# Two-layer recurrent/attention trunk on one Trainium2 core: squares' sums and conditioning rows as one-column matrix products, last gate unit ahead of the last two recurrence blocks, conditioning rows spread over other steps

## The chip, the cores and the metric

The kernel runs on one core of one Trainium2 chip. The core has five engines, each with its own queue: TensorE (PE) multiplies matrices, VectorE (DVE) and ScalarE (ACT) work element by element, GpSimd (POOL) does odd work, and SyncE (SP) issues most of the DMAs. PE writes its results to PSUM, eight banks of 128 x 512 numbers here. The time is the device time of one execution in microseconds; the value shown of a kernel is the median of its runs.

## The reference

Input are `x` (1024 positions x 1024 features, float32), one vector `c` of 1024 numbers, and the parameters. Everything is float32. Layer 0 is a recurrent mixer and an MLP; then one key/value pair is computed; layer 1 is chunked attention and an MLP. What the change touches is the first norm with its conditioning, and the mixer:

```python
c_act = jax.nn.silu(c)
mod = c_act @ ada_w[layer] + ada_b[layer]
sh1, sc1, g1, sh2, sc2, g2 = jnp.split(mod, 6, axis=-1)
hn = modulate(rms_norm(h, norm1_g[layer]), sh1, sc1)
...
z = hn @ w_in
gate, xr = jnp.split(z, 2, axis=-1)
xr = causal_depthwise_conv(xr, conv_w, conv_b)
y = rg_lru(xr, gate_a_w, gate_a_b, gate_x_w, gate_x_b, lam)
return (y * jax.nn.gelu(gate)) @ w_out
```

`rms_norm` divides each position by the root of the mean of its 1024 squares; `modulate` is x * (1 + scale) + shift, with `scale` and `shift` taken from the 6144 numbers `mod`. The mixer is 1408 wide. `rg_lru` works on 16 blocks of 88 features: two 88 x 88 products with sigmoids, elementwise work, and a scan over the 1024 positions. The MLP is `square(relu(hn @ w1)) @ w2`, 4096 wide.

## The kernel before

All activations lie with features on the partitions: eight tiles of 128 features x 1024 positions, each position half 512 wide. Every float32 product is made of three of reduced precision: both operands are split into a high part (written by ACT, `hi`) and a low part (the rest, subtracted by DVE, `lo`), and PE accumulates three products, weight-high x moving-high (L324), weight-high x moving-low (L325) and weight-low x moving-high (L326), in this order. One *unit* is 128 output features: 8 k-tiles x 2 halves x 3 = 48 products of 512 columns.

Weights come through one stream (`ws`). Its items are loaded by SP in order, split by ACT (L191) and DVE (L195), and freed. Conditioning rows are items of that stream too: a *row* is 128 of the 6144 outputs of `mod`, its weights lie as 128 outputs x 1024 inputs, and one DVE instruction (L357) multiplies them by silu(c), broadcast to all partitions as `cb`, and adds up along the row, writing one column of `mods`. Which rows come between which weights is written by hand (`some`, `ada_late`). In the mixer and the first MLP a counter of ticks decides when delayed jobs and low halves are issued (`ws.tick`, `ws.late`, `ws.flush`). The order on each engine is the order of the code there.

**Head.** Squares of x (ACT, L516 and L519) are added up over the eight k-tiles by DVE (L520); four products with a column of ones per half sum them over the partitions (L528); DVE and ACT take the reciprocal root (L533, L619 to L624), DVE writes it on a diagonal (L538), PE broadcasts it (L544), and ACT copies it from PSUM. DVE multiplies x by it (`normed`, L779), ACT applies gain and shift and makes the high half (`moded`, L786 and L788), DVE the low half (`lows`, L792). The 16 rows of scale and shift, two per k-tile, are reduced on DVE (L357) just ahead of their k-tile. Behind this stand the products of the first three units over both halves, 144 of them (`products`).

**Mixer.** For t = 3 to 10: a recurrent unit `xr(t)` with its convolution, the recurrence of the blocks that are complete (`recur`), then a gate unit (`gate(t-1)`). `recur` consists of, per block, 4 x 3 products of 88 x 88 (`gates`; their operands come by DMA and are split at L900 on ACT and L907 on DVE), sigmoids (L933), then tanh, square root and exponential on ACT (L945, L950, L953), and five DVE instructions that end with the scan (L957 to L961). The results go through DRAM (`ygd`) and come back as operands of the output projection, three chunks of k-tiles, whose PSUM banks DVE evicts with the gated residual (L1059).

**First MLP.** Its first four units of `w1` wait for the second norm, hidden tile by hidden tile (`head`; L583 scales, ACT adds the shift and makes the high half, L601 is the low half). The other 28 go in fourteen *quads* of two units (q = 2 to 15), with seven products of half matrices in place of eight; conditioning rows are put between them.

## Time and profile before

| | |
|---|---|
| median of three runs | 2389.01 us (2387.49 to 2394.32) |
| profiled execution | 2395.81 us |
| span of its profile | 2394.0 us |
| mean granted clock of PE | 0.985 |
| PE busy | 2287.7 us |
| DVE busy | 1763.6 us |
| ACT busy | 1246.2 us |

The profiled execution is 6.8 us longer than the median of the runs and has 1.8 us outside its span. In the rows of a timeline the first number is the start in us, the second the duration; then come engine, line, operation, the tile written and the tiles read, the shape and the count; in brackets the idle time of the engine before it and what ended it. In a row of windows each engine has its busy time and its number of instructions, in the order PE, weight loads of PE, DVE, ACT, POOL, followed by the granted clock, the DMA share and GB/s.

### The profile page before, as it was taken

How to read it: one execution, taken by the hardware profiler on the slowest of the kernel's cores; microseconds unless marked ns; L12 is line 12 of the kernel's file. 1: busy time of each engine (PE TensorE's matmuls, PEld its weight loads, DVE VectorE, ACT ScalarE, POOL GpSimd, SP SyncE). 2: the span in 40 equal slices, each digit the busy share in tenths (PEclk: the TensorE clock that was granted, in tenths of full speed). 3: DMA queues.
4: the chain of work that ended last, by engine and by line, in shares of the span. 5: the costliest groups of instructions: out<-in, count | busy, mean ns of one | idle time of the engine just before them, and what ended most of it. 6: DMA issues, size and time to landing. Idle time of an engine off the chain costs nothing.

```text
span 2394.0 us, 31739 instructions
## 1 busy us (share of the span) xinstructions
PE 2287.7 (96%) x11740; PEld 1935.6 (81%) x11740; DVE 1763.6 (74%) x2596; ACT 1246.2 (52%) x2052; POOL 398.7 (17%) x419
## 2 busy tenths in 40 slices
PE   4999989999999899999999999999999999899999
PEld 3778767878877777888999998998888888778887
DVE  8797779588777777778765648997386666778775
ACT  5677873265544643334443229997165555634342
POOL 0001000000000023331000038875000000033322
PEclk9999989999999999999999999999999999999999
DMA  8343349326666774546244200013214444865443
GB/s 306 101 133 106 104 120 314 109 69 220 245 227 236 267 268 147 161 146 228 88 145 131 96 10 10 10 37 122 95 45 165 169 158 163 285 238 161 155 149 133
DMA packets 141640, 363.46 MB, mean 152 GB/s; under 512 B 14924, under 2 KB 17100, under 8 KB 141484
## 3 DMA queue, kind: packets, MB, share of 16 engines
q1 hardware_dynamic: 113756, 278.45, 35.3%
q10 hardware_dynamic: 23824, 71.44, 7.8%
q0 software_dynamic: 3904, 11.54, 1.9%
q8 instruction: 92, 1.51, 0.3%
q14 instruction: 64, 0.52, 0.1%
HBM read 260.19 MB, written 89.65 MB: 146 GB/s over the span
## 4 chain that ended last, share of the span: by engine, by line
PE 65%; DVE 13%; DMA 9%; ACT 8%; issue 4%; POOL 1%; SPq 0%; ACTq 0%; DVEq 0%; POOLq 0%
PE b L325 20%; PE b L326 20%; PE b L324 20%; DMA ws<-in_w_dram 3%; DVE wl L195 2%; DMA hid<-s 2%; PE b L1568 1%; DVE s L195 1%; ACT s L1538 1%; DVE s L357 1%; DMA ws<-hid 1%; ACT s L329 1%; DVE s L1129 1%; POOL ws L123 1%; PE b L1587 1%
## 5 line engine op out<-in xcount | busy, mean ns | idle before, releaser
L324 PE MATMUL b<-s,wh 128*128 128x512 f32 (+1 forms) x2532 | 1004.2, 397 | 43.3 <-DVE s L1231 11.7
L325 PE MATMUL b<-s,wh 128*128 128x512 f32 (+1 forms) x2532 | 998.7, 394 | 19.4 <-DVE s L907 6.5
L326 PE MATMUL b<-s,wl 128*128 128x512 f32 (+1 forms) x2296 | 905.4, 394 | 4.1 <-DVE wl L195 4.1
L324 PEld LDWEIGHTS b<-s,wh 128*128 128x128 f32 (+1 forms) x2532 | 480.0, 190 | 165.0 <-DVE s L1209 13.9
L325 PEld LDWEIGHTS b<-s,wh 128*128 128x128 f32 (+1 forms) x2532 | 479.8, 189 | 128.1 <-DVE s L907 7.4
L191 ACT ACTIVATE wh<-ws 128x1024 fp32r<-128x1024 f32 (+2 forms) x302 | 291.1, 973 | 441.6 <-POOL ws L123 261.1
L326 PEld LDWEIGHTS b<-s,wl 128*128 128x128 f32 (+1 forms) x2296 | 435.1, 190 | 100.1 <-DVE wl L195 5.8
L195 DVE TENSOR_TENSOR wl<-ws,wh 128x1024 fp32r<-128x1024 f32 (+2 forms) x249 | 305.8, 1231 | 113.8 <-ACT wh L191 111.5
L1231 DVE SCALAR_TENSOR_TENSOR s<-b,mod,s 128x512 f32<-128x512 f32 x221 | 165.0, 747 | 88.3 <-PE b L326 88.0
L195 DVE TENSOR_TENSOR s<-ws,s 128x512 fp32r<-128x512 f32 x284 | 223.4, 805 | 0.3 <-ACT s L191 0.3
L123 POOL TENSOR_TENSOR ws<-ws 128x512 f32<-128x512 f32 x21 | 28.4, 1354 | 1165.2 <-DMA s<-hsp 922.3
L324 PE MATMUL b<-wh,s 128*128 128x256 f32 x768 | 216.4, 284 | 0.0
L325 PE MATMUL b<-wl,s 128*128 128x256 f32 x768 | 216.0, 283 | 0.0
L326 PE MATMUL b<-wh,s 128*128 128x256 f32 x768 | 215.2, 283 | 0.5 <-DVE s L562 0.4
L191 ACT ACTIVATE s<-ws 128x512 fp32r<-128x512 f32 x284 | 165.1, 619 | 73.4 <-DMA ws<-ygd 23.7
L325 PEld LDWEIGHTS b<-wl,s 128*128 128x128 f32 x768 | 147.1, 192 | 0.3 <-issue 0.2
L324 PEld LDWEIGHTS b<-wh,s 128*128 128x128 f32 x768 | 147.1, 192 | 0.3 <-issue 0.2
L326 PEld LDWEIGHTS b<-wh,s 128*128 128x128 f32 x768 | 146.5, 192 | 1.0 <-DVE s L562 0.9
L357 DVE CUSTOM_DVE_ANT_0 ws<-ws,cb,vec 128x1024 f32<-128x1024 f32 x59 | 75.3, 1282 | 76.1 <-DMA ws<-in_ada_dram 73.3
L1209 DVE TENSOR_TENSOR s<-s,b 128x512 f32<-128x512 f32 x84 | 57.5, 685 | 99.9 <-PE b L326 88.1
L1207 ACT ACTIVATE s<-b 128x512 f32<-128x512 f32 x84 | 50.0, 596 | 93.2 <-PE b L326 93.0
L1338 ACT ACTIVATE s<-b 128x256 f32<-128x256 f32 x96 | 31.6, 388 | 121.5 <-PE b L326 110.3
(165 smaller groups left out, 3083.7 us busy)
## 6 DMA issues: line engine op xcount, KB each, us to landing
hid<-s ACTq DMA_DIRECT2D x128, 512.0 KB, 5.3
ws<-hid SPq DMA_DIRECT2D x118, 512.0 KB, 4.5
ws<-in_w_dram SPq DMA_DIRECT2D x220, 256.0 KB, 3.4
ws<-in_ada_dram SPq DMA_DIRECT2D x56, 512.0 KB, 3.5
s<-in_ada_dram SPq DMA_DIRECT2D x40, 512.0 KB, 8.8
ws<-in_w_in_dram SPq DMA_DIRECT2D x22, 512.0 KB, 4.6
hsp<-s SPq DMA_DIRECT2D x32, 256.0 KB, 2.0
s<-hsp SPq DMA_DIRECT2D x16, 512.0 KB, 6.9
```

Source lines behind the costliest of these rows:

```text
L123: eng.tensor_tensor(out=out, in0=in0, in1=in1, op=op)
L191: self.nc.scalar.activation(out=hi[:rows, :n], in_=src, func=AF.Copy)
L195: self.nc.vector.tensor_tensor(out=lo[:rows, :n], in0=src, in1=hi[:rows, :n].bitcast(F32), op=ALU.subtract)
L324: PE.matmul(ps, ah, bh, start=start, stop=False, skip_group_check=more)
L325: PE.matmul(ps, ah, bl, start=False, stop=False, skip_group_check=more)
L326: return PE.matmul(ps, al, bh, start=False, stop=stop, skip_group_check=more).ins
L329: A_.activation(out=hi, in_=src, func=AF.Copy)
L357: V.tensor_tensor_reduce(out=t, in0=t, in1=cb, op0=ALU.mult, op1=ALU.add, scale=1.0, scalar=bias, accum_out=dst)
L1207: A_.activation(out=t, in_=ps, func=AF.Copy)
L1209: V.tensor_tensor(out=t, in0=t, in1=ps, op=ALU.add)
L1231: V.scalar_tensor_tensor(out=t, in0=ps, scalar=g2[:, m : m + 1], in1=t, op0=ALU.mult, op1=ALU.add)
L1338: A_.activation(out=d, in_=ps[:, :, e * 128 : (e + 1) * 128], func=AF.Copy)
```

## The change

In the **head** the squares are no longer added up by DVE. Each k-tile's square is multiplied by the column of ones, 4 products per k-tile, all 32 of a half accumulating in one PSUM bank (`sums`). For the conditioning rows of the first norm the weights of a row also exist in another layout (`ada0`: 1024 inputs on the partitions, in eight blocks of 128 x 128), so that eight products with silu(c) as a 128 x 8 tile (`silu`) accumulate one row in one PSUM column (`ada_pe`). Both rows go this way for k = 0, 1, 2, the shift row alone for k = 3 to 7; the scale row of k = 3 to 7 stays on DVE. The load of `cb` and its silu come later.

In the **mixer** the rows between the units are 3, 3, 2 at t = 4, 6, 8 (before 2 each at t = 3 to 6), and the last gate unit (`gate(NT - 1)`) stands ahead of the recurrence of blocks 14 and 15; its weights are loaded ahead of the last gate blocks'. In the **first MLP**, the low halves that are due are written out at the start of each step of the first four units (`ws.flush()`), and the quads carry 0 rows at q = 2 and 15, 2 at q = 3, 8, 13, 14 and 3 elsewhere: 32 instead of 37. The eight rows of the key/value shift go to the **query stage**, four each after the second and third group of weights.

```diff
-        some(2 if t < 7 else 0)
+        some({4: 3, 6: 3, 8: 2}.get(t, 0))
...
     w_in(NT - 2)
+    w_in(NT - 1)
     gate_item(_done(NT - 1))
-    w_in(NT - 1)
...
-            ada_late(0 if l or q == 2 else 2 if q in (3, 15) else 3)
+            ada_late(0 if l or q in (2, 15) else 2 if q in (3, 8, 13, 14) else 3)
...
     for g in range(4):
         for kk in range(2):
             ws.add(I["wq"][g * 2 + kk], 1024)
+        some((0, 4, 4, 0)[g])
...
     load_x(0)
-    nc.sync.dma_start(cb, I["c"].broadcast_to([128, 1024]))
...
     ws.load(3)
+    nc.sync.dma_start(cb, I["c"].broadcast_to([128, 1024]))
...
-    for k in range(KD):
-        n1.sq(k, hs(0))
...
+    def sums(half):
+
+        n1.ps = bank()
+        for k in range(KD):
+            t = slot()
+            A_.activation(out=t[:, :HALF], in_=xt[k][:, hs(half)], func=AF.Square)
+            for j in range(4):
+                PE.matmul(n1.ps[:, j : j + 1], t[:, j * 128 : (j + 1) * 128], ones[:, 0:1],
+                          start=(k, j) == (0, 0), stop=(k, j) == (KD - 1, 3))
+
+    def ada_pe(k):
+
+
+        ps = bank()
+        todo = (1, 0) if k < 3 else (0,)
+        ts = {j: st.pop(0) for j in (1, 0)}
+        for j in todo:
+            for i in range(KD):
+                PE.matmul(ps[:, j : j + 1], ts[j][:, i * 128 : (i + 1) * 128], silu[:, i : i + 1],
+                          start=i == 0, stop=i == KD - 1)
+
+        def out():
+            if k > 2:
+                ada_use(mods[0][:, 8 + k : 9 + k], vc("ab0", 8 + k))(ts[1])
+            for j in todo:
+                V.tensor_tensor(out=mods[0][:, j * 8 + k : j * 8 + k + 1], in0=ps[:, j : j + 1],
+                                in1=vc("ab0", j * 8 + k), op=ALU.add)
+            gain(0, mods[0], 1, vc("n1g0", k), k, 1)
+        return out
...
     gate(NT - 2)
-    recur(_done(NT - 1))
...
     gate(NT - 1)
+    recur(_done(NT - 1))
     load_h(4)
...
+            ws.flush()
             head(k, nrm, l == 0)
```

Added lines push most line numbers up: what is L324, L325, L326 before is L325, L326, L327 after; L195 becomes L196, L357 L358, L520 L521, L544 L551, L601 L608, L907 L938, L957 L988, L1059 L1090. The sums' products are now L779, the rows' L790.

PE, start of the program. Before: four products sum the squares of half 0 (L528), one broadcasts (L544), six are the first k-tile's of two units.

```order
L528 MATMUL b_207<-ones,s_181 128x1 x4
L544 MATMUL b_230<-s_220,ones 128x512
L324 MATMUL b_275<-s_239,wh_222 128x512
L325 MATMUL b_275<-s_240,wh_222 128x512
L326 MATMUL b_275<-s_239,wl_223 128x512
```

After (of the eight rows of L779, which read alike, the last two):

```order
L779 MATMUL b_185<-ones,s_222 128x1 x4
L779 MATMUL b_185<-ones,s_228 128x1 x4
L790 MATMUL b_244<-silu,s_106 128x1 x8
L790 MATMUL b_244<-silu,s_108 128x1 x8
L551 MATMUL b_269<-s_242,ones 128x512
L790 MATMUL b_282<-silu,s_114 128x1 x8
L790 MATMUL b_282<-silu,s_116 128x1 x8
L325 MATMUL b_299<-s_277,wh_261 128x512
L326 MATMUL b_299<-s_278,wh_261 128x512
```

Six more rows of L779, one per k-tile, stand ahead of this piece. The rows of the first two k-tiles stand around the broadcast, ahead of the first 512-column product.

DVE, around the last recurrence (blocks 14 and 15) and the first evictions of the output projection. Before, the first chain of L957 to L961 for these blocks ends ahead of the first eviction L1059:

```order
L957 SCALAR_TENSOR_TENSOR s_2424<-s_2364,s_2424 88x1024
L958 SCALAR_TENSOR_TENSOR s_2364<-s_2364,s_2420 88x1024
L959 TENSOR_SCALAR s_2364<-s_2364 88x1024
L960 TENSOR_TENSOR s_2424<-s_2424,s_2301 88x1024
L961 SCALAR_TENSOR_TENSOR s_2420<-s_2364,s_2424 88x1024
L195 TENSOR_TENSOR s_2459<-ws_1929,s_2459 128x512
L357 ISA ws_2416,mod_82<-ws_2416,cb,vec 128x1024
L357 ISA mod_82 128x1
L357 ISA ws_2418,mod_82<-ws_2418,cb,vec 128x1024
L357 ISA mod_82 128x1
L1059 SCALAR_TENSOR_TENSOR s_2521<-b_2531,mod_82,s_2521 128x512
```

After, four evictions (L1090) stand ahead of that chain, and two more between it and the next one; the last two of the first four, and what follows:

```order
L1090 SCALAR_TENSOR_TENSOR s_2659<-b_2713,mod_82,s_2659 128x512
L196 TENSOR_TENSOR s_2702<-ws_2645,s_2702 128x512
L196 TENSOR_TENSOR s_2705<-ws_2645,s_2705 128x512
L1090 SCALAR_TENSOR_TENSOR s_2661<-b_2732,mod_82,s_2661 128x512
L988 SCALAR_TENSOR_TENSOR s_2653<-s_2594,s_2653 88x1024
L989 SCALAR_TENSOR_TENSOR s_2594<-s_2594,s_2649 88x1024
L990 TENSOR_SCALAR s_2594<-s_2594 88x1024
L991 TENSOR_TENSOR s_2653<-s_2653,s_2443 88x1024
L992 SCALAR_TENSOR_TENSOR s_2649<-s_2594,s_2653 88x1024
L196 TENSOR_TENSOR s_2709<-ws_2680,s_2709 128x512
L196 TENSOR_TENSOR s_2711<-ws_2680,s_2711 128x512
L1090 SCALAR_TENSOR_TENSOR s_2663<-b_2754,mod_82,s_2663 128x512
```

The two chains of the last recurrence have moved behind evictions of the output projection.

DVE, start of the first MLP: the chain of the norm's second half (from L533 to L538, after L540 to L545) and the low halves of the hidden tiles (L601, after L608). Before:

```order
L601 TENSOR_TENSOR s_3408<-s_2523,s_3408 128x512
L583 SCALAR_TENSOR_TENSOR s_2562<-s_2562,aa,s_2529 128x512
L583 SCALAR_TENSOR_TENSOR s_2564<-s_2564,aa,s_2529 128x512
L533 TENSOR_SCALAR q_3480<-b_3475 128x4
L620 RECIPROCAL q_3480<-q_3480 128x4
L621 TENSOR_TENSOR q_3480<-q_3480 128x4
L622 TENSOR_TENSOR q_3480<-q_3480 128x4
L623 TENSOR_SCALAR q_3480<-q_3480 128x4
L624 TENSOR_TENSOR q_3480<-q_3480 128x4
L538 TENSOR_TENSOR s_3488<-ident,q_3480 128x512
L601 TENSOR_TENSOR s_3439<-s_2525,s_3439 128x512
L195 TENSOR_TENSOR wl_3444<-ws_2991,wh_3443 128x1024
```

After:

```order
L608 TENSOR_TENSOR s_3550<-s_2661,s_3550 128x512
L608 TENSOR_TENSOR s_3581<-s_2663,s_3581 128x512
L196 TENSOR_TENSOR wl_3586<-ws_3133,wh_3585 128x1024
L590 SCALAR_TENSOR_TENSOR s_2698<-s_2698,aa,s_2667 128x512
L590 SCALAR_TENSOR_TENSOR s_2700<-s_2700,aa,s_2667 128x512
L540 TENSOR_SCALAR q_3624<-b_3619 128x4
```

The second low half and one weight's low half have moved from behind the chain to ahead of it.

More of the change, by code (lines that the diff above doesn't have):

```diff
@@ L727, in load_ada @@
             t = slot()
-            nc.sync.dma_start(t, ada[0][j * 8 + k])
+            nc.sync.dma_start(t, ada[0][8 + k] if j and k > 2 else I["ada0"][j * 8 + k])
             st.append(t)
     load_x(0)
-    nc.sync.dma_start(cb, I["c"].broadcast_to([128, 1024]))
     load_ada(0)
@@ L762, in trunk @@
     n1 = Norm(xt, aa[:, 0:8], mods[0][:, 0:8])
-    for k in range(KD):
-        n1.sq(k, hs(0))
-    sgm = slot()
-    A_.activation(out=sgm, in_=cb, func=AF.Sigmoid)
-    def ada_k(k):
-        for j in (1, 0):
-            ada_use(mods[0][:, j * 8 + k : j * 8 + k + 1], vc("ab0", j * 8 + k))(st.pop(0))
-        gain(0, mods[0], 1, vc("n1g0", k), k, 1)
-    def sq_b(*ks):
-        for k in ks:
-            n1.sq(k, hs(1))
+    sgm, silu = slot(), cp.tile([128, 8], F32, name="silu")
+    def sums(half):
[22 more added lines that the diff above has]
+        return out
     def normed(half, *ks):
@@ L792, in lows @@
         V.tensor_tensor(out=lo, in0=t, in1=hi.bitcast(F32), op=ALU.subtract)
-    V.tensor_tensor(out=cb, in0=cb, in1=sgm, op=ALU.mult)
-    n1.mm(0)
+    A_.activation(out=silu, in_=vc("c", 0, 8), func=AF.Sigmoid)
+    V.tensor_tensor(out=silu, in0=silu, in1=vc("c", 0, 8), op=ALU.mult)
+    sums(0)
+    n1.roots()
+    adas = [ada_pe(0)]
     ws.pump(2)
     n1.bc(0)
-    ada_k(0)
-    normed(0, 0, 1, 2)
+    adas.pop(0)()
+    normed(0, 0, 1)
     moded(0, 0)
     lows(0, 0)
-    for k in range(4):
-        sq_b(k)
-    ada_k(1)
-    for k in range(4, KD):
-        sq_b(k)
-    moded(1, 0)
-    normed(0, 3)
-    lows(1, 0)
+    adas.append(ada_pe(1))
     hh, hl = n1.hh, n1.hl
@@ L827, in trunk @@
     products((0, 1), 0, 0)
+    adas.pop(0)()
+    moded(1, 0)
+    lows(1, 0)
+    normed(0, 2, 3)
+    sums(1)
+    products((0, 1), 0, 1)
+    n1.roots()
+    adas.append(ada_pe(2))
+    n1.bc(1)
     normed(0, 4, 5)
     ws.pump(3)
-    n1.mm(1)
-    products((0, 1), 0, 1)
-    ada_k(2)
-    n1.bc(1)
+    adas.pop(0)()
     moded(2, 0)
     lows(2, 0)
+    A_.activation(out=sgm, in_=cb, func=AF.Sigmoid)
     unit()
@@ L838, in trunk @@
     products((2,), 0, 1)
+    normed(1, 0, 1, 2)
     products((0, 1, 2), 0, 2)
-    normed(1, 0, 1, 2)
-    normed(0, 6, 7)
     for k in range(3):
         moded(k, 1)
-    ada_k(3)
+    V.tensor_tensor(out=cb, in0=cb, in1=sgm, op=ALU.mult)
     for k in range(3):
         lows(k, 1)
+    adas.append(ada_pe(3))
+    for k in range(3):
         products((0, 1, 2), 1, k)
+    normed(0, 6, 7)
     for k in range(3, KD):
+        adas.pop(0)()
+        normed(1, k)
         moded(k, 0)
+        moded(k, 1)
         lows(k, 0)
-        normed(1, k)
+        lows(k, 1)
         if k < KD - 1:
-            ada_k(k + 1)
-        moded(k, 1)
-        lows(k, 1)
+            adas.append(ada_pe(k + 1))
         products((0, 1, 2), 0, k)
@@ L1684, in put, with units @@
         v[:, o : o + w] = a
+    def units(w, k, n):
+        kk, nn = w.shape
+        return w.reshape(kk // (128 * k), k, 128, nn // n, n).transpose(0, 3, 2, 1, 4).reshape(
+            -1, 128, k * n)
     L["c"] = C(g["c"])
@@ L1690, in layouts @@
         put(f"n2g{l}", col(g["norm2_g"][l]))
+    put("c", col(g["c"][0]))
     put("kvb", col(g["kv_ada_b"]))
```

19 lines of the change are left out of this document (10 added, 9 removed).

## The prediction

> **What bounds the kernel now.** I read the shares of the engines first, then TensorE's own timeline and the windows wherever the change touches it.
>
> ```profile
> span 2394.0 us, 31739 instructions
> PE 2287.7 (96%) x11740; PEld 1935.6 (81%) x11740; DVE 1763.6 (74%) x2596; ACT 1246.2 (52%) x2052; POOL 398.7 (17%) x419
> ```
>
> TensorE (PE) is busy for 96% of the span, so an edit can win only where PE stands idle or runs at a lower granted clock. The change touches five such places: the head (0 to 82 us), the mixer's gate loop, the mixer's end (325 to 443 us), the start of the first MLP, and a few steps of that MLP.
>
> ```profile
> 15.18 1.84 PE L528 MATMUL b<-ones,s 128*128 128x1 f32 x8 [15.18 <-DVE s L520]
> 26.18 0.80 PE L324 MATMUL b<-s,wh 128*128 128x512 f32 x1 [4.79 <-ACT s L788]
> 35.02 1.86 PE L528 MATMUL b<-ones,s 128*128 128x1 f32 x8 [5.61 <-DVE s L520]
> 43.33 0.63 PE L326 MATMUL b<-s,wl 128*128 128x512 f32 x1
> 43.75 0.53 PE L324 MATMUL b<-s,wh 128*128 128x512 f32 x1
> 51.55 0.79 PE L325 MATMUL b<-s,wh 128*128 128x512 f32 x1 [3.47 <-DVE s L792]
> 57.69 0.41 PE L324 MATMUL b<-s,wh 128*128 128x512 f32 x1
> ...
> 52.00:58.00 6.00, 6.00 (x16) 4.60 (x16) 5.05 (x11) 3.30 (x5) 0.00 (x0) 0.53 0.01 3
> 58.00:82.00 24.00, 24.00 (x108) 19.85 (x107) 17.11 (x29) 14.70 (x22) 0.00 (x0) 1.00 0.07 23
> ```
>
> (Of a window the columns are PE, PE's weight loads, DVE, ACT, POOL, then the granted clock.) The head waits for DVE, and its first 43 us are slow: 512-column products follow each other every 0.43 us until 43.75, and after 3.47 us of idling again until 57.69, at a granted clock of 0.53. In the last 24 us PE is never idle, and 108 products take 0.222 us each. So a pause costs twice, once itself and once in the six slow microseconds behind it.
>
> **The change part by part.**
>
> *Head.* DVE loses work, PE gains it. The rows are these, of DVE, of ACT's squares and of eight small records late in the program:
>
> ```profile
> 9.57 5.47 DVE L520 TENSOR_TENSOR s<-s,s 128x512 f32<-128x512 f32 x7
> 21.45 1.28 DVE L357 CUSTOM_DVE_ANT_0 s<-s,cb,vec 128x1024 f32<-128x1024 f32 x1
> 48.33 1.28 DVE L357 CUSTOM_DVE_ANT_0 s<-s,cb,vec 128x1024 f32<-128x1024 f32 x1
> 4.72 0.62 ACT L516 ACTIVATE s<-s 128x512 f32<-128x512 f32 x1
> 7.54 3.29 ACT L519 ACTIVATE s<-s 128x512 f32<-128x512 f32 x5 [0.52 <-DMA s<-in_xT_dram]
> ...
> 1142.00 0.95 PE L528 MATMUL b<-ones,s 128*128 128x1 f32 x8
> ```
>
> Of 14 additions of squares (5.47 us for seven) and 16 row reductions (about 1.2 us apart) only five reductions stay: 10.9 + 13.2 = 24 us of DVE gone. PE gets 64 products for the sums instead of 8, and 88 for the rows: 144 more. The eight records of the row at 15.18 are four products, two records each: 1.84 / 4 = 0.46 us at the low clock; the same eight at full clock took 0.95, so 0.24. The 152 are therefore 36 us at full clock and 70 at the low one. Nothing else grows by so much.
>
> What does PE then do in 82 us? The first square is done at 5.3 and the last at 10.8, and PE's sums follow them. If PE never idled after that and ran at full clock from the first, it would end at 5.3 + 36 + 144 x 0.222 = 73, against 81 now: that is the end of −8. It will not be so. The first sums run at the low clock, 32 x 0.46 = 14.7 us if all of them do and 10 if the clock opens after 6; they end at 16 to 20, about where DVE's sum is ready now (15.2). The first large product still needs root, broadcast, multiplication and activation behind them, 11 us now (15.2 to 26.2) with two reductions of 1.2 us among them that PE takes over. So large products begin at about 26, as before. Behind 26 stand 144 large products, the sums' second half (32 small ones) and 56 small ones for the rows of k = 2 to 7: 144 x 0.222 + 88 x 0.24 = 53 us, so the end is 79 without a pause. The pauses behind 26 are now 5.61 (second sums) and 3.47 (low halves); the squares of the second half, 0.53 us apart on ACT, the chain behind them and the third unit's split leave 4 to 10 us of such time. From k = 3 on, each step is 18 large products and 8 small, 18 x 0.222 + 8 x 0.24 = 5.9 us; before, DVE set the pace there, one step of its list (L779, two L357, two L792) taking 5.3 us:
>
> ```profile
> 58.54 0.68 DVE L779 TENSOR_TENSOR s<-s,s 128x512 f32<-128x512 f32 x1
> 63.87 0.69 DVE L779 TENSOR_TENSOR s<-s,s 128x512 f32<-128x512 f32 x1
> ```
>
> So that last stretch, once bound by DVE with a backlog on PE, becomes bound by PE. Together the end is at 83 to 89, +2 to +8; I take **+5**, with −8 and (below) +32 as ends.
>
> The first of these numbers hangs on the clock being opened by one-column products. [...]
>
> *Mixer's gate loop.* Eight reductions are spread otherwise (3, 3, 2 at t = 4, 6, 8 for 2 each at 3 to 6). The stall there is
>
> ```profile
> 158.41 0.73 PE L325 MATMUL b<-s,wh 88*88 88x512 f32 x1 [5.93 <-DVE s L907]
> ```
>
> and in the new order as many reductions as before, three, stand on DVE behind the scan and ahead of this subtraction: **0**, from −1.2 (one fewer) to +1.2.
>
> *Mixer's end.* The last gate unit's 48 products now stand ahead of blocks 14 and 15.
>
> ```profile
> 331.33 0.39 PE L326 MATMUL b<-s,wl 128*128 128x512 f32 x1
> 337.97 0.73 PE L324 MATMUL b<-s,wh 88*88 88x512 f32 x1 [6.25 <-ACT s L900]
> 350.85 0.58 PE L325 MATMUL b<-s,wh 128*128 128x512 f32 x1
> 351.26 0.39 PE L326 MATMUL b<-s,wl 128*128 128x512 f32 x1
> 370.91 0.50 PE L325 MATMUL b<-s,wh 128*128 128x512 f32 x1 [2.79 <-DVE s L195]
> ...
> 340.48 1.22 DVE L907 TENSOR_TENSOR s<-s,s 88x1024 fp32r<-88x1024 f32 x1 [1.31 <-ACT s L900]
> ...
> 325.00:375.00 50.00, 39.94 (x138) 28.97 (x137) 38.63 (x42) 32.90 (x40) 4.07 (x8) 0.80 0.64 201
> 375.00:443.00 68.00, 68.00 (x301) 56.23 (x301) 58.63 (x81) 15.37 (x22) 0.53 (x1) 1.00 0.74 255
> 348.00:443.00 95.00, 91.73 (x388) 74.23 (x387) 78.41 (x104) 34.01 (x45) 2.66 (x5) 0.96 0.72 245
> ```
>
> From 375 on a product takes 68 / 301 = 0.226 us; the 138 of the first window would need 31.2 of its 50 us. Some 18.8 us are lost: 6.25 and 0.53 idle, 2.79 idle before the out-projection, and the clock (0.43 us spacing from 337.97 to 351). The gate unit, 48 x 0.226 = 10.9 us, covers the conversion of blocks 14 and 15, ready at 340.48 + 1.22 = 341.7: 331.5 + 10.9 = 342.4. So the pause and its slow stretch, about 6.8 + 6 us, are free to go. But DVE does 78.4 us of work from 348 to 443, and has to do nearly all of it in the new order too, now with two chains of the recurrence (L957 to L961, 6.6 us each) queued among the evictions L1059 that give PE its PSUM banks back. DVE was late even before, until here:
>
> ```profile
> 359.73 0.96 DVE L195 TENSOR_TENSOR wl<-ws,wh 128x768 fp32r<-128x768 f32 x1 [6.37 <-ACT wh L191]
> 363.62 1.22 DVE L957 SCALAR_TENSOR_TENSOR s<-s,s 88x1024 f32<-88x1024 f32 x1
> 367.98 2.29 DVE L961 TENSOR_TENSOR_SCAN s<-s,s 88x1024 f32<-88x1024 f32 x1
> 425.57 2.21 DVE L1059 SCALAR_TENSOR_TENSOR s<-b,mod,s 128x512 f32<-128x512 f32 x3
> 432.46 0.75 DVE L1059 SCALAR_TENSOR_TENSOR s<-b,mod,s 128x512 f32<-128x512 f32 x1 [1.97 <-PE b L326]
> ```
>
> Three evictions back to back at 425.57 are a backlog; at 432.46 DVE waits for PE again. With PE 13 us earlier, DVE reaches that point no earlier than its own work lets it: its idle time in the window is 95 − 78.4 = 16.6 us, of which 6.37 is one wait for a weight that ACT converts behind the exponentials, and that wait stays in some form. So at most 10 to 13 us can come through, and with a chain of 6.6 us ahead of an eviction PE, which has eight banks and fills one in 12 x 0.226 = 2.7 us, waits a few times for 1 to 5 us. I take **−5**, with −13 and +4 (both scans, less the banks' cover, on top of an unchanged wait for ACT) as ends.
>
> *Start of the first MLP.* The low halves of two hidden tiles are written together, ahead of the chain of the second normalization.
>
> ```profile
> 494.43 0.67 PE L325 MATMUL b<-s,wh 128*128 128x512 f32 x1 [3.45 <-DVE s L601]
> 498.93 0.16 DVE L533 TENSOR_SCALAR q<-b 128x4 f32<-128x4 f32 x1 [3.23 <-PE b L528]
> 500.98 0.68 DVE L601 TENSOR_TENSOR s<-s,s 128x512 fp32r<-128x512 f32 x1
> 501.72 0.80 PE L325 MATMUL b<-s,wh 128*128 128x512 f32 x1 [2.49 <-DVE s L601]
> 503.32 2.13 DVE L123 TENSOR_TENSOR ws<-ws,ws 128x512 f32<-128x512 f32 x3
> ```
>
> The tile of the row at 500.98 was held up by the chain that begins at 498.93. Ahead of it, it is written about 494.5, and the stall of 2.49 us goes; the one at 494.43 stays. The next tile's low half comes behind the chain and four additions (L123), three of which take 2.13 us, and PE may wait for it a little. Less idle time means a shorter slow stretch too. **−3**, from −4 to 0.
>
> *Steps of the first MLP.* Reductions leave steps 8, 13, 14 and 15; of those, PE waited for DVE notably only in step 13:
>
> ```profile
> 745.34 0.50 PE L324 MATMUL b<-s,wh 128*128 128x512 f32 x1 [1.62 <-DVE s L1209]
> ```
>
> One reduction of 1.28 us fewer: **−1.5** with step 14's share, from −2 to 0. The long waits at the second matrix's start are not touched.
>
> *Query stage.* The eight reductions that left the MLP and the mixer's share land here, 8 x 1.2 = 10 us of DVE where PE has little idle time; two of them stand between the third normalization's root and its broadcast. **+1**, from 0 to +2.5.
>
> *Sum:* 5 + 0 − 5 − 3 − 1.5 + 1 = −3.5 us. The profiled execution took 2395.8 us (span 2394.0 and 1.8 around it), so 2392.3 for one like it; it lies 6.8 over the median of the runs shown, 2389.0, so **2385.5** against that median.
>
> **The rivals.**
>
> *The mixer's end keeps all of its gain* (faster). If ACT converts the last out-projection weights early enough and DVE's idle 16.6 us are usable, the term is −13 instead of −5, and the head, relieved of 24 us of DVE, ends at 81 to 83, +1. The sum is 1 − 13 − 3 − 1.5 + 1 = −15.5: 2373.5. For it speaks that PE's pause of 6.25 us at 337.97 goes for certain; against it, the backlog at 425.57.
>
> *One-column products do not open the clock* (slower). The mechanism sits in the head: records of one column stand in this trace in eights only, and no row shows whether the granted clock rises during a long run of them, as it does under large products. If it does not, all 152 take 0.46 us, 70 us for 36. Even with every large product at full clock the head ends at 5.3 + 70 + 32 + 6 (pauses) = 113, 32 us late: sum +23.5, 2412.5. It decides the sign as soon as the small products cost more than 3.5 + 7.2 = 10.7 us over my value, that is, if about a third of them run slow. [...]
>
> *The scans block the banks* (slower, a little). At the mixer's end the term is +4, the head +8: sum +8.5, 2397.5. For it: the two chains of 6.6 us; against: DVE's idle time.
>
> That the change does not do what it says can be left aside except for the gate loop, where the new spread leaves three reductions at the same place; that is in the sum as 0.
>
> **How the numbers follow.** Forecast, within a few microseconds of 2385: 0.40. Full gain at the mixer's end: 0.32. Clock not opened: 0.15. Scans block: 0.13. A measurement here tells about 0.3%, 7.2 us, from no change. From the forecast's own spread (2378 to 2393) a little falls under −7.2 us: faster 0.32 + 0.04 = 0.36; slower 0.15 + 0.10 (most of the last case) + 0.01 = 0.26; the rest, 0.38, within 0.3%. The range goes from 2370, a little under the full gain, to 2412, which leaves out the worst half of the clock's case; the forecast's own is 2378 to 2393.
>
> **What would show it.** Head: the last large product of the first units ends at 83 to 89 (now 81); eight records of L779 (the sums' line in the changed kernel) in about 0.95 us from 12 us on, and a spacing of 0.23 between the large ones at 26; if eight still take 1.84 at 30 us, the clock's rival holds. Mixer's end: no idle time of PE between 331 and 350, and waits for L1090 (the evictions' new line) between 355 and 430, and the last evictions of the second chunk about 5 us earlier once the head's shift is taken off. First MLP: only one stall of 3.45 us on the low half (L608). Step 13: its 1.62 us gone. Wrong would be: a stall in a place that I put at nothing, above all the gate loop or the query stage, or a head that ends before 81.

## The result, and the profile after

The changed kernel took 2408.63 us (median of four runs, 2406.47 to 2414.57) where the kernel before took 2390.18 (four runs, 2387.49 to 2394.32): a ratio of 1.008 with a 95% interval of 1.0055 to 1.0104. It is slower by 18.45 us, clear of the noise; the forecast was 2385.5, and the price of its rival "one-column products do not open the clock" was 2412.5. The profiled execution took 2414.57 us with a span of 2412.8, the longest of the four.

Of the page of the changed kernel, the span, the busy times, and DVE's busy tenths in forty slices of the span:

```profile
span 2412.8 us, 32314 instructions
PE 2335.8 (97%) x12028; PEld 1987.1 (82%) x12028; DVE 1745.5 (72%) x2572; ACT 1242.7 (52%) x2053; POOL 399.1 (17%) x419
DVE  2678878679777787778766548998376566777775
```

PE has 288 records more (a *record* is one entry of PE in the trace; a small product leaves two) and is busy 48.1 us longer, in a span that is 18.8 us longer; DVE is busy 18.1 us less, and its first slice (60 us) has fallen from 8 tenths to 2. So PE lost some 29 us of idle time and got 48 us more of busy time. Where that lies is in PE's timeline of the head of the changed kernel (start, duration, then the group):

```profile
6.96 13.78 PE L779 MATMUL b<-ones,s 128*128 128x1 f32 x64 [6.96 <-ACT s L777]
20.60 6.97 PE L790 MATMUL b<-silu,s 128*128 128x1 f32 x32
27.43 2.05 PE L551 MATMUL b<-s,ones 128*128 128x512 f32 x2
29.27 6.83 PE L790 MATMUL b<-silu,s 128*128 128x1 f32 x32
35.96 0.77 PE L325 MATMUL b<-s,wh 128*128 128x512 f32 x1
36.53 0.63 PE L326 MATMUL b<-s,wh 128*128 128x512 f32 x1
38.67 13.72 PE L779 MATMUL b<-ones,s 128*128 128x1 f32 x64
54.95 6.82 PE L790 MATMUL b<-silu,s 128*128 128x1 f32 x32
71.77 1.84 PE L790 MATMUL b<-silu,s 128*128 128x1 f32 x16
...
104.30 0.78 ACT L910 ACTIVATE s<-b,vec 128x512 f32<-128x512 f32 x1 [1.25 <-PE b L327]
```

64 records in 13.78 us are 0.215 us each, from 7 us to 20; the same spacing, 6.82 / 32 = 0.213, still holds from 55 to 62. Only behind a run of 512-column products (from 65.32 on) does a record take 1.84 / 16 = 0.115, at 71.77. The first large product comes at 35.96 instead of 26.18, and ACT's first conversion of a finished unit at 104.30 instead of 77.65: 26.65 us later.

The ledger below takes the same instruction in each trace and gives how much later it is than in the trace before. "Only the rest" is the run with all parts but the head (E1), "128 columns" the changed kernel with wider small products (E2), "corrected" the fastest kernel (E9).

| instruction | before | after | only the rest | 128 columns | corrected |
|---|---|---|---|---|---|
| first conversion of a recurrent unit (end of the head) | 77.65 | +26.65 | −0.9 | +2.0 | −0.8 |
| first gate sigmoid | 111.15 | +23.4 | −5.4 | −1.5 | −4.9 |
| last conversion of a recurrent unit | 318.08 | +23.5 | −6.0 | −2.1 | −5.0 |
| last eviction of the output projection | 489.65 | +21.0 | −9.3 | −4.8 | −13.8 |
| fourth addition of the quads | 573.67 | +19.4 | −10.6 | −6.3 | −15.5 |
| first eviction of the second matrix | 833.56 | +11.4 | −19.8 | −14.9 | −24.3 |
| 103rd eviction of the second matrix | 1123.20 | +12.4 | −21.0 | −17.9 | −26.5 |
| its last eviction (query stage's norm) | 1152.19 | +17.9 | −17.5 | −13.6 | −26.9 |
| span | 2394.0 | +18.8 | −16.8 | −11.2 | −28.2 |

One caution on such differences: behind the head, eight of the kernels run here have the same code, and from the first conversion to the end they took 2297.6 to 2308.5 us in their profiled executions (2308.5 is the changed kernel's). The trace before is that of an execution some 6 us above its median, too. A term of a few microseconds is therefore read from several traces or not at all.

### The profile page after: what moved, and what is told of

Its sections match the earlier page's. It is cut to its first block, busy times and chain, and to the rows that moved or that the text cites. A ratio compares the mean times of both kernels' runs of the same rounds, so it can differ in the third digit from the quotient of the medians.

```text
span 2412.8 us, 32314 instructions
## 1 busy us (share of the span) xinstructions
PE 2335.8 (97%) x12028; PEld 1987.1 (82%) x12028; DVE 1745.5 (72%) x2572; ACT 1242.7 (52%) x2053; POOL 399.1 (17%) x419
## 4 chain that ended last, share of the span: by engine, by line
PE 67%; DVE 12%; DMA 8%; ACT 7%; issue 4%; POOL 1%; SPq 0%; ACTq 0%; DVEq 0%; POOLq 0%
PE b L325 20%; PE b L327 20%; PE b L326 20%; DMA ws<-in_w_dram 4%; DVE s L196 2%; DVE wl L196 2%; PE b L1600 1%; ACT s L1570 1%; PE b L790 1%; DVE ws L124 1%; PE b L779 1%; ACT s L330 1%; POOL ws L124 1%; DVE s L358 1%; DMA hid<-s 1%
## 5 line engine op out<-in xcount | busy, mean ns | idle before, releaser
L325 PE MATMUL b<-s,wh 128*128 128x512 f32 (+1 forms) x2532 | 1003.7, 396 | 37.8 <-DVE s L1263 10.3
L326 PE MATMUL b<-s,wh 128*128 128x512 f32 (+1 forms) x2532 | 996.2, 393 | 10.4 <-DVE s L938 6.5
L327 PE MATMUL b<-s,wl 128*128 128x512 f32 (+1 forms) x2296 | 904.0, 394 | 2.8 <-DVE wl L196 2.7
L325 PEld LDWEIGHTS b<-s,wh 128*128 128x128 f32 (+1 forms) x2532 | 479.3, 189 | 157.7 <-ACT wh L192 10.7
L326 PEld LDWEIGHTS b<-s,wh 128*128 128x128 f32 (+1 forms) x2532 | 479.4, 189 | 115.6 <-DVE s L938 7.0
L327 PEld LDWEIGHTS b<-s,wl 128*128 128x128 f32 (+1 forms) x2296 | 434.8, 189 | 99.4 <-DVE wl L196 5.0
L196 DVE TENSOR_TENSOR wl<-ws,wh 128x1024 fp32r<-128x1024 f32 (+2 forms) x249 | 305.4, 1230 | 126.9 <-ACT wh L192 124.7
L196 DVE TENSOR_TENSOR s<-ws,s 128x512 fp32r<-128x512 f32 x284 | 227.3, 817 | 1.2 <-ACT s L192 1.2
L325 PE MATMUL b<-wh,s 128*128 128x256 f32 x768 | 216.5, 284 | 0.0
L326 PE MATMUL b<-wl,s 128*128 128x256 f32 x768 | 216.0, 283 | 0.0
L327 PE MATMUL b<-wh,s 128*128 128x256 f32 x768 | 215.1, 284 | 0.8 <-DVE s L569 0.8
L327 PEld LDWEIGHTS b<-wh,s 128*128 128x128 f32 x768 | 146.3, 192 | 1.5 <-DVE s L569 1.2
L325 PEld LDWEIGHTS b<-wh,s 128*128 128x128 f32 x768 | 147.1, 192 | 0.3 <-issue 0.2
L326 PEld LDWEIGHTS b<-wl,s 128*128 128x128 f32 x768 | 147.1, 192 | 0.3 <-issue 0.2
L358 DVE CUSTOM_DVE_ANT_0 ws<-ws,cb,vec 128x1024 f32<-128x1024 f32 x64 | 81.3, 1281 | 75.0 <-DMA ws<-in_ada_dram 73.3
```

Source lines behind the costliest of these rows:

```text
L196: self.nc.vector.tensor_tensor(out=lo[:rows, :n], in0=src, in1=hi[:rows, :n].bitcast(F32), op=ALU.subtract)
L325: PE.matmul(ps, ah, bh, start=start, stop=False, skip_group_check=more)
L326: PE.matmul(ps, ah, bl, start=False, stop=False, skip_group_check=more)
L327: return PE.matmul(ps, al, bh, start=False, stop=stop, skip_group_check=more).ins
L358: V.tensor_tensor_reduce(out=t, in0=t, in1=cb, op0=ALU.mult, op1=ALU.add, scale=1.0, scalar=bias, accum_out=dst)
```

## The experiments

The theory after the result: the loss is the head's, and there it is the clock, which one-column products neither open nor keep open. (The clock is *open* when the granted clock is 1.00, and low when it is 0.50.) Rivals: the small products cost what they cost by their number, whatever the clock; or the parts share a cause.

**E1, all parts but the head.**

Its head is the kernel before's (`load_ada`, the squares, `ada_k` and their order; no `sums`, no `ada_pe`, no `ada0`); all else is as changed.

> All parts of the change except the head, whose code is that of the kernel before. Theory (the loss sits in the head alone): the trace after shows the head 26.65 us later and everything behind it 7.85 us shorter; 3.2 of these come right behind the head and may belong to it, so 4.6 to 7.9 us faster than before, 2382 to 2386. Rival (the parts share one cause, for instance DVE being later everywhere because of the head's order): no gain without the head, 2390 within 3 us.

Measured: 2378.15 us (2376.71 to 2379.02), a ratio of 0.9936 (0.9921 to 0.9951) to the kernel before. The parts other than the head win 15 us, more than the 4.6 to 7.9 expected and nearly twice the 8.5 that the prediction's terms sum to. The trace after had shown only 7.85 us of it, since that execution was the slowest behind the head.

**E12, the head alone.**

It is the kernel before with the head of the changed kernel and nothing else.

> The kernel before with the new head alone. Theory (the loss sits in the head, and the rest of the change adds its gain beside it): the head's first conversion at 104.3 as with the whole change, 26.65 later than before, and that much, within 4 us of noise, in the time: 2412 to 2421 against some 2390. Rival (the head with its lighter DVE and other loads changes what the later parts are worth): under 2410 or over 2424.

Measured: 2415.22 us (2412.63 to 2424.04), a ratio of 1.0125 (1.0088 to 1.0163): 24.4 us slower. The loss is the head's. The two runs do not add up to the whole, though: −15 and +24 are +9, and the change measured +18. The medians of the kernel before, 2389.55 to 2393.04 from one set of runs to the next, explain a part; the rest stays open. The head's first conversion came at 97.3 in this execution, not at the 104.3 written down, and the trace shows why:

```profile
6.96 13.79 PE L778 MATMUL b<-ones,s 128*128 128x1 f32 x64 [6.96 <-ACT s L776]
35.97 0.77 PE L325 MATMUL b<-s,wh 128*128 128x512 f32 x1
38.67 10.62 PE L778 MATMUL b<-ones,s 128*128 128x1 f32 x64
51.86 3.91 PE L789 MATMUL b<-silu,s 128*128 128x1 f32 x32
```

The second 64 records took 10.62 us, the first 13.79: behind the six large products from 35.97 the clock was open for a time in this execution, and was not in the one of the changed kernel (13.72 us for the same records). With 0.115 and 0.215 us a record, 10.62 us are 31 fast ones and 33 slow ones: by this estimate it stayed open for about 3.6 us of one-column products. That may be part of the spread of these kernels' runs.

**E2, E4 and E11, wider small products.** Only the number of moving columns changes; the weights, their number and the order stay. The first of the equal columns is used, and the instructions that read it are moved to its place.

```diff
-                PE.matmul(n1.ps[:, j : j + 1], t[:, j * 128 : (j + 1) * 128], ones[:, 0:1],
+                PE.matmul(n1.ps[:, j * 128 : j * 128 + W], t[:, j * 128 : (j + 1) * 128], ones[:, 0:W],
...
-                PE.matmul(ps[:, j : j + 1], ts[j][:, i * 128 : (i + 1) * 128], silu[:, i : i + 1],
-                          start=i == 0, stop=i == KD - 1)
+                PE.matmul(ps[:, j * 128 : j * 128 + W], ts[j][:, i * 128 : (i + 1) * 128],
+                          silu[:, i : i + 1].broadcast_to([128, W]), start=i == 0, stop=i == KD - 1)
```

> The changed kernel, but every small product multiplies by 128 equal columns in place of one (the sums by 128 columns of ones, the rows by silu's column repeated); the result's first column is used. As many products, as many weight loads. Theory (one-column products leave the clock low, and 128 columns are enough to open it): eight records take about 1.0 us instead of 1.73 from some 6 us after the first, the first large product comes at 26 to 30 instead of 35.96, and the head ends 18 to 25 us earlier: 2384 to 2391. Rival (the small products cost what they cost by their weight loads, whatever the clock): same times or longer ones, 2408 to 2415.

> As with 128 columns, with 32 in place of 128. If the clock goes by how much of the time columns move: 32 columns fill about an eighth of a record's 0.215 us at the low clock and the clock stays low, 2408 within 4 us. If any stream of more than a few columns opens it: as with 128, 2384 to 2391.

> As the run with 128 columns per small product, with 64 in place of 128. If the clock goes by the share of time in which columns move (64 columns fill a quarter of a record's 0.215 us at the low clock): it opens at times, or later than with 128, first large product between 24 and 36. If the threshold lies under 64: as with 128, first large product at 24.

Measured: W = 128 took 2380.71 us (0.995, 0.9935 to 0.9966), less than the 2384 to 2391 written down, W = 32 took 2402.74 (1.0044, 1.0025 to 1.0063; its ten runs spread from 2396.93 to 2415.68), W = 64, in one run, 2391.27. PE's timeline with 128 columns, and then with 64:

```profile
6.93 9.15 PE L779 MATMUL b<-ones,s 128*128 128x128 f32 x64 [6.93 <-ACT s L777]
15.92 3.74 PE L790 MATMUL b<-silu,s 128*128 128x128 f32 x32
23.84 0.47 PE L325 MATMUL b<-s,wh 128*128 128x512 f32 x1
26.56 7.41 PE L779 MATMUL b<-ones,s 128*128 128x128 f32 x64 [0.97 <-ACT s L777]
```

```profile
7.05 13.89 PE L779 MATMUL b<-ones,s 128*128 128x64 f32 x64 [7.05 <-ACT s L777]
20.73 7.03 PE L790 MATMUL b<-silu,s 128*128 128x64 f32 x32
36.06 0.77 PE L325 MATMUL b<-s,wh 128*128 128x512 f32 x1
38.77 7.50 PE L779 MATMUL b<-ones,s 128*128 128x64 f32 x64
```

128 times the arithmetic, and the head ends at 79.62 instead of 104.30. With 128 columns the first 64 records take 9.15 us, 0.143 each, so the clock opened on the way, and 32 records then take 3.74, 0.117 each. With 64 columns the first 29 us stayed at 0.217 a record, but after the large products at 36 the clock was open and stayed so (7.50 for 64, 0.117 each). With 32, the profiled execution went like the one-column kernel, 13.84 and 13.81 us for its two halves; but the median lies 6 us under the changed kernel's and below the 2404 to 2412 written down, so that its other executions may have gone otherwise. What costs the time is thus not the number of products or of weight loads, which is the same in all three. The rival falls. 128 columns opened the clock; 64 did not open it in the one execution looked at, but kept it open; 32 did not open it in theirs, and as no open clock stood ahead of a long run of them, whether they keep one open is not shown.

**E3, the clock opened beforehand.**

```diff
+    warm = bank()
+    for i in range(6):
+        PE.matmul(warm, ones, ones.unsqueeze(1).broadcast_to([128, 4, 128]), start=True, stop=True)
     sums(0)
     n1.roots()
```

> The changed kernel with six additional 512-column products on the tile of ones ahead of the sums, in the 7 us in which TensorE is idle; their result is not read. If large products open the clock and one-column products keep it open: all sums at about 0.115 us a record, the head 18 to 25 us earlier, 2384 to 2391. If one-column products count as idle time, the clock closes again within some microseconds of sums: a gain of at most 5 us, 2403 to 2409. Rival (the clock is not the cause): no gain, 2408 or up to 3 more.

Measured: 2405.41 us (1.0056, 1.0037 to 1.0075). The windows of PE right behind the six products (PE's busy time and number of records first, the granted clock third from the end):

```profile
8.00:10.00 2.00, 2.00 (x18) 1.81 (x17) 1.29 (x10) 1.99 (x5) 0.00 (x0) 1.00 1.03 397
10.00:12.00 2.00, 2.00 (x19) 2.00 (x18) 0.00 (x0) 1.68 (x2) 0.00 (x0) 0.91 1.02 418
12.00:14.00 2.00, 2.00 (x11) 2.00 (x11) 0.00 (x0) 0.00 (x0) 0.00 (x0) 0.50 1.02 416
14.00:16.00 2.00, 2.00 (x11) 2.00 (x11) 0.00 (x0) 0.00 (x0) 0.00 (x0) 0.50 1.04 415
```

PE is without a gap in these eight microseconds, and yet the clock falls from 1.00 to 0.50: by estimate, the mean of 0.91 from 10 to 12 puts the fall at about 11.6, some 3.4 us after the last large product, whose successor starts at 8.19. In this run the stream of one-column products did not keep the clock open. That is the second outcome of the three written down, with its gain of at most 5 us.

**E10, the pauses of the old head filled** (on E1): 5, 9 and 6 products of 512 columns on the tile of ones behind the first broadcast, ahead of the second sums, and ahead of the second half's products.

```diff
     n1.bc(0)
+    idle(5)
...
     products((0, 1), 0, 0)
+    idle(9)
     normed(0, 4, 5)
...
+    idle(6)
     for k in range(3):
         lows(k, 1)
         products((0, 1, 2), 1, k)
```

> All parts of the change but the head, with twenty additional 512-column products on the tile of ones in the head: 5 behind the first broadcast, 9 ahead of the second half's sums, 6 ahead of the second half's products. Their result is not read. Theory (of the old head's time a part is the low clock behind each pause): with the pauses filled, the products from 52 on take 0.23 us instead of 0.43, and the head's first conversion comes 2 to 4 us earlier, 73 to 75 in place of 76.72; 2374 to 2377. Rival (DVE's list sets that time, or the additional products delay the real ones as much as they help): 76 to 79, 2378 to 2382.

Measured: 2378.47 us, against 2378.15 for E1: no difference that shows. The head's end moved from 76.72 to 76.52, although the clock was open. The same two windows, of E1 and then of E10:

```profile
52.00:58.00 6.00, 6.00 (x22) 4.82 (x22) 5.05 (x11) 3.29 (x5) 0.00 (x0) 0.79 0.01 1
58.00:82.00 24.00, 24.00 (x106) 19.65 (x105) 18.40 (x30) 15.87 (x24) 0.00 (x0) 1.00 0.07 23
```

```profile
52.00:58.00 6.00, 6.00 (x27) 4.78 (x26) 5.05 (x10) 3.10 (x5) 0.00 (x0) 1.00 0.01 1
58.00:82.00 24.00, 23.90 (x106) 19.41 (x105) 18.39 (x30) 16.06 (x24) 0.00 (x0) 1.00 0.07 23
```

27 records in place of 22, and next to nothing of it arrives. The additional products delayed the real ones by half a microsecond at 52; that DVE's list, the same in both, sets the end fits this. In E1 the slow stretch was short, however: the kernel before had 16 records in that window, at 0.53, and its head ended at 77.65. In the other kernels with the old head 18 to 21 records went with 77.11 to 76.60. So the slow stretch behind the pause, which the prediction counted as a second price, cost at most about 1 us.

**E7, fewer rows on TensorE** (on E2): both rows of k = 3 to 7 on DVE.

```diff
-        todo = (1, 0) if k < 3 else (0,)
+        todo = (1, 0) if k < 3 else ()
...
```

> The changed kernel with 128 columns per small product, and both rows of k = 3 to 7 on DVE again (rows of k = 0 to 2 and all sums stay on TensorE). Theory (with the clock open the head is bound by TensorE's own work, 16 records of 0.12 us less per step): the head's first conversion at 75 to 77 in place of 79.62, 2376 to 2379. Rival (DVE paces these steps at 5.3 us again, and later): head at 79 to 82, 2380 to 2384.

Measured: 2388.91 us (0.9985, 0.9973 to 0.9998). The head's first conversion came at 84.78, later than the 79.62 with the shift rows on PE and than the 76.72 of the old head, and later than either outcome written down. Five rows of some 1.2 us on DVE cost 5.2 us. DVE is not full there, busy 19.1 of the 26 us from 58 on: DVE and ACT wait for each other in turn. ACT's activation waits for the gain that DVE makes from the rows, DVE's low half for the activation, and the next rows stand behind it in DVE's order. One such round takes 6.1 us (ACT starts at 61.52, 67.61 and 73.70), and PE, which has no pause there in E2, waits 1.2 us and more in each.

**E5, the rows of the MLP's quads alone.**

```diff
-            ada_late(0 if l or q == 2 else 2 if q in (3, 15) else 3)
+            ada_late(0 if l or q in (2, 15) else 2 if q in (3, 8, 13, 14) else 3)
...
             ws.add(I["wq"][g * 2 + kk], 1024)
+        some((0, 5, 0, 0)[g])
```

> The kernel before with the new number of rows in the MLP's quads alone; the five rows that leave them go to the query stage. Theory (from the two traces, by the same evictions: the stretch from quad 4 to the first sums of the second matrix is 8.3 us shorter after the change, and the query stage 5.5 longer, for eight rows there): 7 to 9 us less in the quads and the turn to the second matrix, 2 to 4 more in the query stage, 2385 to 2389 against some 2392. Rival, my prediction's term (one reduction of 1.28 us in step 13 and a part in step 14): 1 to 2 us less in the quads, and the turn to the second matrix unchanged, 2390 to 2393.

Measured: 2383.19 us (0.9965, 0.9952 to 0.9978), 7.4 us faster, a little under the 2385 to 2389 written down. Its trace is 2.3 us early at the quads' fourth addition, 12.6 at the first eviction of the second matrix. So 10 us of this trace come from an edit that the prediction valued at 1.5. Over all traces the same stretch takes 259.9 and 257.6 us without the edit (before, E12) and 248.5 to 254.4, 251.3 in the mean, in the twelve with it: about 7 us, as much as the medians show. They come mostly at the turn from the first matrix to the second. DVE there, before and after the change:

```profile
816.83 0.69 DVE L123 TENSOR_TENSOR ws<-ws 128x512 f32<-128x512 f32 x1 [5.45 <-DMA ws<-in_w_dram]
819.50 1.22 DVE L195 TENSOR_TENSOR wl<-ws,wh 128x1024 fp32r<-128x1024 f32 x1
```

```profile
827.88 0.69 DVE L124 TENSOR_TENSOR ws<-ws 128x512 f32<-128x512 f32 x1 [2.31 <-DMA ws<-in_w_dram]
830.54 1.22 DVE L196 TENSOR_TENSOR wl<-ws,wh 128x1024 fp32r<-128x1024 f32 x1
```

The wait for the second matrix's first quad fell from 5.45 to 2.31 us. The SP queue says what stood ahead of that load: before, two rows, and then six loads of hidden tiles that wait for slots, until 806.59; the same load is issued at 820.68 after, when everything else is 18 us later.

```profile
770.50 0.90 SPq L156 DMA_DIRECT2D s<-in_kvada_dram  x2
780.55 25.79 SPq L156 DMA_DIRECT2D ws<-hid  x6
806.59 3.21 SPq L156 DMA_DIRECT2D ws<-in_w_dram  x4
```

```profile
795.30 25.13 SPq L157 DMA_DIRECT2D ws<-hid  x6
820.68 3.21 SPq L157 DMA_DIRECT2D ws<-in_w_dram  x4
```

Counted from the additions around 754, which are 18.1 us late after the change, the load is 4 us earlier. Rows were priced as DVE instructions; at this place they were loads and slots.

**E6, the query stage's eight rows under the second matrix instead** (on E1).

```diff
             ws.add_quad(*(I["w2"][l][s % 4][x][:, c] for x in range(4)), 512, G if s > 1 else V)
+            ada_late(0 if l or not 4 <= s < 12 else 1)
...
-        some((0, 4, 4, 0)[g])
```

> All parts of the change but the head, with the eight rows of the query stage moved to steps 4 to 11 of the first MLP's second matrix, one each. Theory (the query stage pays for its eight rows, and DVE has room under the second matrix): the stall of 2.42 us ahead of the broadcast at 1126 goes, 3 to 4.5 us less than with the rows in the query stage, 2373 to 2376. Rival (the query stage's loss has another cause, or the rows cost as much under the second matrix): 2378 within 2 us.

Measured: 2385.7 us (0.9978, 0.9963 to 0.9993), 7.5 us slower than E1, worse than either outcome written down. The stall ahead of the broadcast went, as expected, but between the first and the 103rd eviction of the second matrix the lead fell from 22.4 to 11.8 us. Eight rows cost 10.6 there, more than their own 1.2 us each. DVE is idle for 62 of the 270 us from 840 to 1110, but that is not the room the theory wanted: a row ahead of an eviction keeps PE from its bank, and PE waited for evictions five more times than in E1, the longest these:

```profile
908.31 0.50 PE L324 MATMUL b<-s,wh 128*128 128x512 f32 x1 [2.26 <-DVE s L1233]
1030.77 0.50 PE L324 MATMUL b<-s,wh 128*128 128x512 f32 x1 [2.92 <-DVE s L1233]
```

What the eight rows do in the query stage is seen in the changed kernel's DVE and PE:

```profile
1157.31 0.16 DVE L631 TENSOR_TENSOR q<-q 128x4 f32<-128x4 f32 x1
1158.77 1.28 DVE L358 CUSTOM_DVE_ANT_0 ws<-ws,cb,vec 128x1024 f32<-128x1024 f32 x1 [1.30 <-DMA ws<-in_kvada_dram]
...
1159.98 0.69 DVE L545 TENSOR_TENSOR s<-ident,q 128x512 f32<-128x512 f32 x1
...
1160.72 2.07 PE L551 MATMUL b<-s,ones 128*128 128x512 f32 x2 [3.32 <-DVE s L545]
```

The root is ready at 1157.5. Then a row stands in DVE's queue whose weights have not landed: 1.30 us of waiting and 1.28 of work ahead of the diagonal, and PE stands for 3.32 us. With five rows in place of eight (E5, E9) no row stood between the root and the diagonal, and PE did not wait there; E5's query stage got 0.6 us longer, not the 2 to 4 written down.

**E8, the rows of the output projection's first chunk in the gate loop** (on E1).

```diff
-        some({4: 3, 6: 3, 8: 2}.get(t, 0))
+        some({4: 3, 5: 2, 6: 3, 7: 2, 8: 2, 9: 2, 10: 2}.get(t, 0))
...
-            some((2, 2, 0)[c])
+            some((0, 2, 0)[c])
```

> All parts of the change but the head, with the eight rows of the output projection's first chunk moved into the mixer's gate loop (two each at t = 5, 7, 9, 10). Theory (the mixer's end is bound by DVE's work, so that the gate unit's gain was mostly lost): DVE has about 9.6 us less to do there, PE's waits for evictions (1.07, 4.61 and 1.76 us) shrink, the last eviction comes 4 to 9 us earlier unless the gate loop gets later by as much: 2370 to 2375. Rival (the two scans ahead of evictions make these waits, whatever else DVE does): the waits stay, 2378 to 2381.

Measured: 2374.21 us (0.9926, 0.99 to 0.9952). From the last unit's conversion to the last eviction the trace is 7.7 us shorter than before the change; E1 was 3.3. So DVE's work bounds a part of that stretch. PE's two waits there remained, 2.88 and 3.57 us, so the scans' place costs as well: each theory has a part. The rows at t = 5 and 7 took 3.9 us of it back at the first gate sigmoid (109.66 against 105.75).

**E9, corrected** (on E1): the rows later in the gate loop, five rows in the query stage.

```diff
-        some({4: 3, 6: 3, 8: 2}.get(t, 0))
+        some({4: 3, 6: 3, 8: 3, 9: 3, 10: 4}.get(t, 0))
...
-            some((2, 2, 0)[c])
+            some((0, 2, 0)[c])
...
-        some((0, 4, 4, 0)[g])
+        some((0, 5, 0, 0)[g])
```

> All parts of the change but the head, with two corrections from the runs so far: the eight rows of the output projection's first chunk stand late in the mixer's gate loop (3, 3, 3, 3, 4 rows at t = 4, 6, 8, 9, 10), and five rows stand in the query stage in place of eight. Theory (DVE bounds the mixer's end; the rows at t = 5 and 7 delayed the first recurrence; with five rows no stall stood ahead of the query stage's broadcast): the first gate sigmoid at 106, the last eviction at 476, no wait for the diagonal at 1125, 2368 to 2373. Rival (DVE's work is only shifted, and the last gate blocks wait for it instead): 2375 to 2380.

Measured: 2370.34 us (2367.59 to 2372.88), a ratio of 0.9919 (0.9904 to 0.9934): 19 us faster than the kernel before, with its old head. It has the lowest median of all. First sigmoid 106.29, last eviction 475.82 and no wait for the diagonal, as written down.

## Why the prediction was wrong

**The head: +5 forecast, +26.65 in the profile.** The arithmetic of the step was right, its price was the wrong one of the two. The prediction had both, 0.24 us for a source product at the high clock and 0.46 at the low one, and took 36 us for the 152, as if the clock opened under the first sums. That is the step that failed: 64 records took 13.78 us, and even the last of a long stream took 0.215 each. At 0.215 for 224 records and 0.115 for the last 80, from k = 3 on, where the clock is open (large products 0.23 us apart from 71.07 on), the 152 products took about 57 us: 21 over the 36, close to the term's error of 21.65. At the low price for all, 70 us, the rival put the head 32 us late; it came 26.65 late. It had the small products 13 us too dear, and gave a part of that back by taking every large product at the high clock: some 24 of them ran at the low one, 0.43 us apart, too. So the mechanism of the rival was right and its size 5 us too large. The chance of 0.15 was too small for a question which the trace before left open and on which 34 us hung. With 128 columns in place of one the head's first conversion is at 79.62, 2 us later than before: with the clock open the term would have been about +2, the lower end of the forecast's +2 to +8.

That one-column products open the clock, on which the 36 us rested, no run shows. In its place the runs showed 29 us of one-column records with one broadcast among them (6.96 to 35.96) that stayed at 0.215 us a record, and an open clock that was lost, by estimate, after 3.4 to 3.6 us of such records (E3, E12).

**The old head: "a pause costs twice".** Wrong in size: the second price was about 1 us at most. E10 filled the pauses, the clock was open, and the head ended 0.2 us earlier than in E1 and 1.1 earlier than before.

**The gate loop: 0 forecast, −3.3 in the profile.** The stall at 158.41 stayed, as forecast (6.54 us after the change). The gain lies at a place that the prediction passed over, the first recurrence, where PE waited before the change:

```profile
109.41 0.73 PE L324 MATMUL b<-s,wh 88*88 88x512 f32 x1 [2.47 <-ACT s L873]
```

The chain there begins with copies between partitions, issued by POOL. Their DMA issue, of before and of E1 (the group's count, its size, and the time from issue to landing):

```profile
s<-s POOLq DMA_DIRECT2D x1, 352.0 KB, 8.6
```

```profile
s<-s POOLq DMA_DIRECT2D x1, 352.0 KB, 4.5
```

Before, two loads of rows were issued by SP in the same stretch; in E1 one, later. That the loads make the copies slow fits both traces, but was not tried by itself, and E12 speaks against it as the whole cause: it has the old spread and two loads of rows in the same stretch, and yet its copies took 5.4 us, and the first sigmoid came 30.3 us after the head's first conversion, as against 33.5 before and 29.0 in E1. The cause stays open.

**The mixer's end: −5 forecast, −2.5 in the profile, −3.3 in E1.** Right in kind: the pause of 6.25 us and its slow stretch went, and DVE gave most of it back. Of the changed kernel, PE's waits for the evictions and the window that holds them:

```profile
404.02 0.47 PE L325 MATMUL b<-s,wh 128*128 128x512 f32 x1 [2.75 <-DVE s L1090]
413.00 0.79 PE L325 MATMUL b<-s,wh 128*128 128x512 f32 x1 [3.01 <-DVE s L1090]
...
400.00:450.00 50.00, 43.87 (x172) 34.92 (x171) 49.90 (x66) 10.62 (x14) 1.61 (x3) 0.90 0.80 268
```

DVE is busy 49.90 of 50 us. The wait for ACT's weights, held to stay in some form, was gone, but rows and the two chains stood ahead of evictions, and PE waited for these. The failed step is the idle time of DVE, of which the prediction held 10 to 13 us usable: from the last conversion to the last eviction DVE was idle for 40 us before and for 38 after, so only 2 to 3 were used. One wait is new, ahead of the first eviction and of the full stretch:

```profile
386.87 0.75 DVE L1090 SCALAR_TENSOR_TENSOR s<-b,mod,s 128x512 f32<-128x512 f32 x1 [3.87 <-DMA s<-in_xT_dram]
```

It is for the tiles of x that the residual needs; SP issues their loads only from 379.32 on, as the code has them behind the moved recurrence. Every kernel with the moved gate unit has this wait (3.26 us in E1, 5.84 in E8, 5.54 in E9), and the kernel before does not. Loading x earlier was not tried.

**The first MLP's start: −3 forecast, −1.6 in the profile, −1.4 in E1.** The stall of 2.49 us went, the one of 3.45 stayed. The part on the clock had the wrong sign in this execution: before, two slow stretches of some 3.5 and 2.7 us (large products 0.43 us apart from 494.43 and from 501.72) stood behind the two stalls; now the one behind 515.43, at a granted clock of 0.50, lasts until 524.56, 9.1 us.

```profile
515.43 0.80 PE L326 MATMUL b<-s,wh 128*128 128x512 f32 x1 [3.45 <-DVE s L608]
519.01 1.70 PE L529 MATMUL b<-ones,s 128*128 128x1 f32 x8
524.56 0.45 PE L325 MATMUL b<-s,wh 128*128 128x512 f32 x1
```

The eight one-column records at 519 lie in that stretch, at 0.21 each. Other executions with the same pause differ: in E11 no slow stretch follows its 3.46 us (the granted clock stays at 1.00).

**The MLP's quads: −1.5 forecast, −8.0 in the profile, −10 in E5, −7 over all traces.** The sentence that failed is "the long waits at the second matrix's start are not touched". They were: the edit also took two loads out of the queue ahead of the second matrix's weights.

**The query stage: +1 forecast, +5.5 in the profile, +3.5 in E1.** The place was right, though one row, not two, stood between root and diagonal. The size was not, as only its work was counted and not its wait for its own load. (Of the eight rows five came from the quads and three from the key/value stage behind; the mixer's number stayed the same.)

Outside the head the terms sum to −8.5, and E1 measured −15; the profile of the whole change shows −7.85. The head's error, 21.65 us in the profile, is what put the time outside the forecast's own range of 2378 to 2393; the wide range, up to 2412, held it only by the clock's rival, and the sign was forecast wrongly.

## What to carry to other kernels

Before work is moved to TensorE as narrow products, ask which clock it will run at: price it at the low one (0.215 us a record here) unless wide products run among them as here from k = 3 on (512 columns; 0.115 us a record). If a narrow product must come first, try it with its column repeated, which here cost next to nothing a record (0.117 us with 128 columns against 0.115 with one, both with the clock open) and won 28 us with 128 columns. A row, or any small item of a load stream, is to be priced three times, as an instruction, as a load that stands ahead of others, and as a wait in the queue of the engine that it reaches.
